# A two-layer decoder trunk: the norm on ScalarE, transposed activations split in PSUM, 128-row rotary scores and one-tensor roots

## The chip, the cores and the metric

The kernel runs on one core of a Trainium2 chip. A core has five engines with queues of their own: TensorE (PE, with its weight loads shown as PEld), VectorE (DVE), ScalarE (ACT), GpSimd (POOL) and SyncE (SP), which here issues most of the transfers. The metric is the device time of one execution in microseconds (us); lower is better.

## The reference

One sequence of 1024 tokens with 1024 features goes through two layers. A layer is a token mixer and a channel mixer. Both are wrapped in the same way, with a shift, a scale and a gate worked out from a vector `c`:

```
x <- LayerNorm(alpha * x + (1 + gate) * sublayer(x * (1 + scale) + shift))
```

The mixer of layer 0 is latent attention: 8 heads, queries and keys through low-rank latents, each head with 128 plain and 64 rotary dimensions, and the rotary key shared by all heads:

```python
s = (jnp.einsum('bqhd,bkhd->bhqk', qn, k_nope)
     + jnp.einsum('bqhr,bkr->bhqk', qp, k_pe)).astype(jnp.float32) * scale
s = jnp.where(causal, s, jnp.float32(-1e30))
p = jax.nn.softmax(s, axis=-1).astype(v.dtype)
return jnp.einsum('bhqk,bkhd->bqhd', p, v)
```

The mixer of layer 1 is a diagonal complex state-space layer (S5): an input projection, a recurrence over the tokens, GELU, a gated unit and an output projection. The channel mixer is the same in both layers, with 4096 hidden features:

```python
a = jax.nn.relu(h @ w1 + b1)
return (a * a) @ w2 + b2
```

Everything is float32.

## The kernel before, in words

**Precision.** Every large product is made of three. A float32 operand is split into `hi`, its rounding to the format in which TensorE takes one pass, and `lo`, the rest; `mm3` (lines 77 to 80, three matmuls on L78, L79 and L80) adds hi·hi, hi·lo and lo·hi in one PSUM bank. A split is a copy into `hi` on ScalarE and a subtraction into `lo` on VectorE (`split`, L74 and L75).

**Tiling.** The 1024 tokens are eight tiles of 128 rows; tile t holds every eighth token from t. `X[t]` is a 128 x 1024 tile in SBUF, the running activation. For a product over features the activation must be transposed: `hT[I]` is a pair (hi, lo) of 128 x 8 x 512 tiles, features on the partitions, 8 blocks of 128 features, 512 tokens (four tiles). `T5["h"]` is the same for the input of the state-space layer.

**Order.** The program is written for a framework that schedules it: it simulates a timeline and gives each engine its own instruction order, so that the order of the program text decides among what is ready. TensorE then takes its instructions strictly in that order. The mixer and other background work are Python generators, advanced by `step(...)`; the order in which the text calls them is written by hand. PSUM has eight banks of 512 columns after the attention: two for transposes (`psT`, tag `tr`), two for `a1` (first products of the channel mixer) and four for `mm` (output products).

**Stages on the timeline.** Setup and modulation vectors run to about 104 us. The attention runs to about 410. `score(h, i)` adds five matmuls for each stretch of keys: three by `mm3` for the plain part, and two for the rotary part (L723 and L724). For the rotary part, `st` and the tiles `kE` and `kO` are 128 rows high: 64 rows of hi and 64 of lo, in opposite order in `kE` and `kO`. L723 uses all 128 rows (hi·lo and lo·hi); L724 uses the 64 rows `r` that hold hi·hi.

Then comes the output projection of the attention, tile by tile (`o_stage`, `o_tiles`, and `o_end`, which adds the residual on L950 and calls the norm), to about 507. The channel mixer `mlp(0, ...)` with `finish0` follows: pairs of hidden blocks `mm1` and `mm2`, with weights loaded and split as it goes (`load1`, `load2`). From about 1222 to 1268 the last pass `mm2(js, h)` overlaps with the norm and the transposes for the state-space layer, whose input projection (`u_strip`, weights `wi` by `u_load`) follows. From 1490 the gated unit and output projection run, then `mlp(1, ...)` with `finish1` from about 1670 to the end at 2408.

**The norm.** `stats(t)` takes mean and variance of a tile on VectorE (`bn_stats`, `bn_aggr`) and makes 1/sqrt by `rsqrt` (L115 to L131): a shift, a first guess on the bits, and two refinements, all on one number per partition; the tiles `bmv` hold the mean and `bny` the root. `norm(t)` then applies (x − mean)·root in one VectorE instruction (L850). The gain and offset of the LayerNorm are in two places: folded into `acol` and `bcol` (with scale and shift), which are applied after the transpose, and in the rows `ra`, `rb`, by which GpSimd multiplies and adds (`residual`, L868 and L869) to make the next running activation.

**The transposes.** `to_hT(t, n, ...)` handles one token tile. For each half of the feature blocks it takes one PSUM bank, transposes four 128 x 128 blocks by TensorE (L857), applies `acol` and `bcol` by four ScalarE instructions from PSUM into an SBUF tile `ht` (L861), copies `ht` to `hi` (L864: on VectorE for the first half, on ScalarE for the second) and subtracts into `lo` on VectorE (L865). `half_dst` says where the result goes.

In layer 0, tiles 0 to 3 are transposed one by one as their norms are done; after the eighth, the loop near L1340 does tiles 4 to 7 with `step(mixer, t > 5)` between them. In `finish0` each tile is transposed, updated and stored to memory (`x_d`) when its norm is done. In layer 1, four tiles are done after tile 3 and four after tile 7. At the end, `finish1` handles the last eight tiles: 0 to 5 by `accumulate` (L841 is the addition in `stats`, L824 the one in `accumulate`), `norm` and `residual`; 6 and 7 by four instructions on VectorE (L1494, L1495), so that the last stores leave early.

Of the kernel before, what the change touches and what calls it, by code (L numbers as in the profile page):

```python
# [9 lines left out]
F32 = mybir.dt.float32  # L10
F32R = mybir.dt.float32r
I32 = mybir.dt.int32
AF = mybir.ActivationFunctionType
ALU = mybir.AluOpType
# [25 lines left out]
def kernel(  # L40
# [29 lines left out]
    def f32(ap):  # L70
        return ap.bitcast(F32)
# [43 lines left out]
    def rsqrt(v, y, tmp, ti):  # L115

        def vyy():
            if v.shape[-1] == 1:
                V.scalar_tensor_tensor(tmp, v, y, y, ALU.mult, ALU.mult)  # L119
            else:  # L120
                V.tensor_tensor(tmp, v, y, ALU.mult)
                V.tensor_tensor(tmp, tmp, y, ALU.mult)

        V.tensor_scalar(ti, v.bitcast(I32), 1, None, ALU.logical_shift_right)
        V.tensor_scalar(y.bitcast(I32), ti, -1.0, 1597463007.0, ALU.mult, ALU.add)
        vyy()
        V.scalar_tensor_tensor(y, tmp, -3.0, y, ALU.add, ALU.mult)
        vyy()
        V.scalar_tensor_tensor(tmp, tmp, -40.0 / 3.0, tmp, ALU.add, ALU.mult)
        V.tensor_scalar(tmp, tmp, 80.0, -3.0 / 256.0, ALU.add, ALU.mult)  # L130
        V.tensor_tensor(y, y, tmp, ALU.mult)  # L131
# [574 lines left out]
    def score(h, i):  # L706
        I = i // 4
        w = (i + 1) * 128
        ps = ps_s[i % 2].tile([128, 1024], F32, tag="s", name="s")
        qsl = slice((i % 4) * 128, (i % 4) * 128 + 128)  # L710
        qh, ql = Q[h, I]
        st = ST[h, I]
        for cc in range((w + 511) // 512):
            n = min(512, w - 512 * cc)
            if n == 128:
                n = 256
            o = ps[:, 512 * cc:512 * cc + n]
            kh, kl = K_[h, cc]
            mm3(o, qh[:, qsl], ql[:, qsl], kh[:, 0:n], kl[:, 0:n], True, False)
            ks, kx = (kE, kO) if h % 2 == 0 else (kO, kE)  # L720
            r = slice(0, 64) if h % 2 == 0 else slice(64, 128)
            ksl = slice(512 * cc, 512 * cc + n)
            PE.matmul(o, st[:, qsl], ks[:, ksl], start=False, stop=False)  # L723
            PE.matmul(o, st[r, qsl], kx[r, ksl], start=False, stop=True)  # L724
        d = ps[:, i * 128:i * 128 + 128]
        V.tensor_tensor(d, d, cmask, ALU.add)
        mx = ap3.tile([128, 4], F32, tag="mx", name="mx", bufs=4)
        V.reduce_max(mx[:, 0:1], ps[:, 0:w], axis=AX.X)
        V.tensor_scalar(mx[:, 1:2], mx[:, 0:1], -SM_SCALE, None, ALU.mult)
        p = ap3.tile([128, w], F32, tag=f"p{i}", name="p", bufs=1)  # L730
        S.activation(p, ps[:, 0:w], AF.Exp, bias=mx[:, 1:2], scale=SM_SCALE, accum_out=mx[:, 2:3])
        V.reciprocal(mx[:, 3:4], mx[:, 2:3])
        if i < 2:
            P.tensor_scalar(p, p, mx[:, 3:4], 0.0, ALU.mult, ALU.add)
        else:
            S.activation(p, p, AF.Copy, scale=mx[:, 3:4])
        PT[h, i] = p
# [94 lines left out]
    def stats(t, add=None):  # L832

        st = cst.tile([128, 2, 6], F32, tag="bst", name="bst", bufs=2)
        mv = cst.tile([128, 2], F32, tag="bmv", name="bmv", bufs=2)
        y = cst.tile([128, 4], F32, tag="bny", name="bny", bufs=2)
        ti = cst.tile([128, 1], I32, tag="bni", name="bni", bufs=2)
        for h in range(2):
            xh = X[t][:, h * 512:h * 512 + 512]
            if add is not None:  # L840
                V.tensor_tensor(xh, xh, add[h], ALU.add)  # L841
            V.bn_stats(st[:, h], xh)
        V.bn_aggr(mv, st.rearrange("p a b -> p (a b)"))
        V.tensor_scalar(y[:, 0:1], mv[:, 1:2], LN_EPS, None, ALU.add)
        rsqrt(y[:, 0:1], y[:, 1:2], y[:, 2:3], ti)
        return mv[:, 0:1], y[:, 1:2]

    def norm(t):

        V.tensor_scalar(X[t], X[t], *stats(t), ALU.subtract, ALU.mult)  # L850

    def to_hT(t, n, wp, dst, tile=None):

        for k0 in (0, 4):
            ps = (tile or tr_tile)()
            for k in range(4):
                PE.transpose(ps[:, k * 128:k * 128 + 128], X[t][:, (k0 + k) * 128:(k0 + k + 1) * 128], ident)  # L857
            h = wp.tile([128, 4, 128], F32, tag="r2", name="ht", bufs=4)
            for k in range(4):
                a, b, src = acol[:, n, k0 + k:k0 + k + 1], bcol[:, n, k0 + k:k0 + k + 1], ps[:, k * 128:k * 128 + 128]  # L860
                S.activation(h[:, k], src, AF.Identity, bias=b, scale=a)  # L861
            for hi, lo, view in dst(t, k0):
                hv = view(h)
                (S.activation(hi, hv, AF.Copy) if k0 else V.tensor_copy(hi, hv))  # L864
                V.tensor_tensor(lo, hv, f32(hi), ALU.subtract)  # L865

    def residual(t, ra, rb):
        P.tensor_tensor(X[t], X[t], ra, ALU.mult)  # L868
# [19 lines left out]
    def out_weight(wp, src, gate, k, hi, lo, eng=None):  # L888
# [2 lines left out]
        SY.dma_start(r, src[k * 128:(k + 1) * 128, :])  # L891
        (eng or V).tensor_tensor(r, r, gate, ALU.mult)
        split(hi, lo, r)

    def half_dst(A):
        def dst(t, k0):
            hi, lo = A[t // 4]
            sl = slice((t % 4) * 128, (t % 4) * 128 + 128)
            return [(hi[:, k0:k0 + 4, sl], lo[:, k0:k0 + 4, sl], lambda h: h)]
        return dst  # L900

    def o_tiles(lhs, w, k_outer=False):

# [43 lines left out]
    def o_end(t, ps):  # L947
        for h in range(2):
            xh = X[t][:, h * 512:h * 512 + 512]
            V.scalar_tensor_tensor(xh, xh, ALPHA, ps[h], ALU.mult, ALU.add)  # L950
        norm(t)
        if t < 4:
            to_hT(t, 0, wp, half_dst(hT))
            residual(t, ra, rb)


# [120 lines left out]
    for t in range(2, 8):  # L1077
        ps = o_tiles([nxt], WO.__getitem__, t == 7)[0]
        if t < 7:
            nxt = o_stage(t + 1)  # L1080
            o_end(t, ps)
    hT[1] = [pa1.tile([128, 8, 512], F32R, tag="pa", name="hT") for _ in range(2)]
    for p_ in wo_p[::-1]:
        p_.release()
    pb = pool("pb", bufs=4)
# [246 lines left out]
    def finish0(t, ps):  # L1332
        accumulate(t, ps)
        if t == 0:
            step(bg, 1000)
            T5["rows"] = res_rows(wp, ln_ffn_g[0], ln_ffn_b[0])
            q = [p_.tile([128, 8, 512], F32R, tag=g, name="h5") for p_, g in ((pa2, "pa"), (pa2, "pa"), (pa1, "pa"), (pb, "pb"))]
            T5["h"] = [q[0:2], q[2:4]]
        norm(t)
        to_hT(t, 1, wp, half_dst(T5["h"]))  # L1340
        residual(t, *T5["rows"])
        SY.dma_start(x_d[t], X[t])
        if t == 5:
            u_load(0)

    mixer = mlp(0, hT, cont, gffn, wp, bg, finish0, w1x, pace=0.6)
    next(mixer)
    o_end(7, ps)
    for t in range(4, 8):
        to_hT(t, 0, wp, half_dst(hT), mm_half)  # L1350
        residual(t, ra, rb)
        step(mixer, t > 5)
    step(mixer, 100)


# [125 lines left out]
    def finish1(t, ps):  # L1481
        if t == 0:
            T5["rows"] = res_rows(wp, ln_ffn_g[1], ln_ffn_b[1], al=1.0)
        g, b = T5["rows"]
        if t < 6:
            accumulate(t, ps)
            norm(t)
            residual(t, g, b)
            SY.dma_start(outr[t], X[t])
            return  # L1490
        mu, rs = stats(t, ps)
        for h in range(2):
            sl = slice(h * 512, h * 512 + 512)
            V.scalar_tensor_tensor(X[t][:, sl], X[t][:, sl], mu, g[:, sl], ALU.subtract, ALU.mult)  # L1494
            V.scalar_tensor_tensor(X[t][:, sl], X[t][:, sl], rs, b[:, sl], ALU.mult, ALU.add)  # L1495
            SY.dma_start(outr[t][:, sl], X[t][:, sl])
# [3 lines left out]
    for t0, n in ((0, 3), (3, 1), (4, 1), (5, 1), (6, 1), (7, 1)):  # L1500
        for t, ps in zip(range(t0, t0 + n), o_tiles([z_of(t) for t in range(t0, t0 + n)], WO.__getitem__, n > 1)):
            accumulate(t, ps)
            norm(t)
            if t % 4 == 3:
                hT[t // 4] = [pb.tile([128, 8, 512], F32R, tag="pb", name="hT") for _ in range(2)]
                if t == 7:
                    cont = containers(pa_tiles([128, 4096], F32R, "ct"))
                    w1x = tuple(wp.tile([128, 8, 128], F32R, tag=g, name="w1x", bufs=1) for g in ("k4", "a4"))
                    mixer = mlp(1, hT, cont, gffn, wp, iter(()), finish1, w1x)
                    next(mixer)  # L1510
                for t_ in range(t - 3, t + 1):
                    to_hT(t_, 2, wp, half_dst(hT), mm_half if t == 7 else None)
                    residual(t_, ra, rb)
                    step(mixer, t_ > 5)
    step(mixer, 100)
    for p_ in (pb, wp, psM, psA, psT, pa2, xp, pa1, drm, cst):
        p_.release()
# [31 lines left out]
```

## Time and profile before

| | |
|---|---|
| three runs | 2406.59, 2409.71 (median), 2413.19 us |
| the profiled execution | 2409.98 us |
| its span, from the first to the last instruction | 2408.0 us |
| mean granted TensorE clock | 0.971 |
| TensorE busy | 2276.5 us (95%), 11039 matmuls |
| VectorE busy | 1522.6 us (63%), 2660 instructions |
| ScalarE busy | 816.9 us (34%), 1457 instructions |
| GpSimd busy | 555.3 us (23%), 550 instructions |
| memory traffic | 190.88 MB read, 34.54 MB written, mean 94 GB/s |

The profile is of one execution. Busy times are the sums of the instructions' durations on an engine. In the lines shown below, a line of a timeline begins with the start and the duration in us, then the engine, the source line (L857), the operation, output <- inputs with their names, and in brackets the idle time before it and what ended it. A line of waits reads: who <- whom, the microseconds waited in all, how often, the longest. A line by source has minimum, median and maximum duration in ns. A line of the costliest groups has the count, the busy time in us, the mean ns of one, and the idle time before them.

### The profile page before, as it was taken

What the parts mean: (1) busy time and instruction counts of PE and PEld (TensorE: products, weight loads), DVE (VectorE), ACT (ScalarE), POOL (GpSimd) and SP (SyncE); (2) the same over time, 40 slices, a digit from 0 to 9 for tenths busy, and PEclk for the clock granted to TensorE, in tenths of its full rate; (3) what the DMA queues carried; (4) which work ended last, traced back from release to release, by engine and by line L of the source; (5) the groups of instructions that cost most, each with busy time, mean ns of one, the idle gap of its engine ahead of it and who ended that gap; (6) DMA issues with size and microseconds to landing.
All of it is one profiled execution on the core that took longest, in us unless ns stands there. A gap on an engine that the chain in (4) does not pass through costs nothing. (4 is left out here: it accounts for less than half of the span.)

```text
span 2408.0 us, 29142 instructions
## 1 busy us (share of the span) xinstructions
PE 2276.5 (95%) x11039; PEld 1885.7 (78%) x11039; DVE 1522.6 (63%) x2660; ACT 816.9 (34%) x1457; POOL 555.3 (23%) x550
## 2 busy tenths in 40 slices
PE   7799998889999999999996999998999999999995
PEld 6666776767888888888886998877788888888884
DVE  8777677977767766666467436379444444444439
ACT  3466665432222333333233233324222222222220
POOL 5623557430000234333024111015000000000004
PEclk9899999989999999999997999999899999999998
DMA  7211224126453344446114545330121111111201
GB/s 255 68 50 56 69 62 158 70 70 198 154 155 110 92 123 142 123 119 161 48 49 158 156 153 173 114 97 20 60 62 44 44 53 44 61 45 36 62 27 70
DMA packets 191289, 229.41 MB, mean 95 GB/s; under 512 B 45329, under 2 KB 136732, under 8 KB 189102
## 3 DMA queue, kind: packets, MB, share of 16 engines
q1 hardware_dynamic: 186270, 214.98, 29.1%
q0 software_dynamic: 3840, 12.59, 1.7%
q8 instruction: 86, 1.41, 0.2%
q14 instruction: 53, 0.43, 0.1%
q10 hardware_dynamic: 1040, 0.00, 0.0%
HBM read 190.88 MB, written 34.54 MB: 94 GB/s over the span
## 5 line engine op out<-in xcount | busy, mean ns | idle before, releaser
L824 DVE TENSOR_TENSOR X<-X,mm 128x512 f32<-128x512 f32 x490 | 330.4, 683 | 269.5 <-PE mm L80 265.7
L868 POOL TENSOR_TENSOR X<-X,ra 128x1024 f32<-128x1024 f32 x30 | 79.0, 2636 | 909.8 <-DVE X L850 667.9
L78 PE MATMUL mm<-pb 128*128 128x512 f32 x512 | 203.9, 399 | 5.4 <-DVE X L824 5.3
L78 PE MATMUL mm<-ct 128*128 128x512 f32 x512 | 199.4, 390 | 1.5 <-DVE X L824 1.5
L79 PE MATMUL mm<-pb 128*128 128x512 f32 x512 | 200.3, 391 | 0.0
L80 PE MATMUL mm<-pb 128*128 128x512 f32 x512 | 200.3, 391 | 0.0
L79 PE MATMUL mm<-ct 128*128 128x512 f32 x512 | 199.7, 390 | 0.0
L80 PE MATMUL mm<-ct 128*128 128x512 f32 x512 | 198.5, 389 | 0.0
L78 PE MATMUL a<-hT,ct 128*128 128x512 f32 x496 | 194.3, 392 | 2.9 <-DVE ct L1018 2.9
L78 PE MATMUL a<-hT,pb 128*128 128x512 f32 x496 | 194.9, 393 | 0.0
L1015 ACT ACTIVATE a<-a,vt 128x512 f32<-128x512 f32 x128 | 83.3, 651 | 327.5 <-PE a L80 327.4
L80 PE MATMUL a<-hT,pb 128*128 128x512 f32 x496 | 194.3, 392 | 0.0
L80 PE MATMUL a<-hT,ct 128*128 128x512 f32 x496 | 193.9, 391 | 0.0
L79 PE MATMUL a<-hT,ct 128*128 128x512 f32 x496 | 193.9, 391 | 0.0
L79 PE MATMUL a<-hT,pb 128*128 128x512 f32 x496 | 193.8, 391 | 0.0
L995 DVE TENSOR_TENSOR w2r<-w2r,gffn 128x1024 f32<-128x1024 f32 x64 | 83.0, 1297 | 138.5 <-DMA w2r<-in_mlp_w_dram 138.5
L78 PEld LDWEIGHTS mm<-pb 128*128 128x128 f32 x512 | 96.4, 188 | 27.3 <-DVE X L824 7.4
L78 PEld LDWEIGHTS mm<-ct 128*128 128x128 f32 x512 | 96.3, 188 | 21.7 <-DVE X L824 1.9
L80 PEld LDWEIGHTS mm<-pb 128*128 128x128 f32 x512 | 96.4, 188 | 20.4
L79 PEld LDWEIGHTS mm<-ct 128*128 128x128 f32 x512 | 96.4, 188 | 20.1
L78 PEld LDWEIGHTS a<-hT,ct 128*128 128x128 f32 x496 | 93.8, 189 | 23.2 <-DVE ct L1018 3.6
L80 PEld LDWEIGHTS mm<-ct 128*128 128x128 f32 x512 | 96.2, 188 | 20.0
(476 smaller groups left out, 5390.1 us busy)
## 6 DMA issues: line engine op xcount, KB each, us to landing
w1r<-in_mlp_w_dram SPq DMA_DIRECT2D x64, 512.0 KB, 4.7
w2r<-in_mlp_w_dram SPq DMA_DIRECT2D x64, 512.0 KB, 4.5
pt<-prm_d SPq DMA_DIRECT2D x16, 1536.0 KB, 7.6
prm_d<-cb SPq DMA_DIRECT2D x80, 128.0 KB, 2.4
wm<-in_mod_mix_w_dram SPq DMA_DIRECT2D x8, 1024.0 KB, 11.7
mb<-in_mod_ffn_w_dram POOLq DMA_DIRECT2D x32, 256.0 KB, 3.1
mb<-in_mod_ffn_w_dram SPq DMA_DIRECT2D x32, 256.0 KB, 2.9
mr<-in_mod_ffn_w_dram SPq DMA_DIRECT2D x32, 256.0 KB, 3.4
```

What stands on the lines that cost most here:

```text
L78: PE.matmul(ps, lh, rh, start=start, stop=False)
L79: PE.matmul(ps, lh, rl, start=False, stop=False)
L80: PE.matmul(ps, ll, rh, start=False, stop=stop)
L824: V.tensor_tensor(xh, xh, ps[h], ALU.add)
L868: P.tensor_tensor(X[t], X[t], ra, ALU.mult)
L995: V.tensor_tensor(r, r, gate, ALU.mult)
L1015: S.activation(ps, ps, AF.Relu, bias=vt2[:, l * 32 + j:l * 32 + j + 1])
```

## The change

1. **Rotary scores (L724).** The second rotary matmul takes all 128 rows of `st` and `kx` instead of the 64 rows `r`; the other 64 rows add the product lo·lo.
2. **Roots.** For one number per partition, `rsqrt` is written with `tensor_scalar` alone: one tensor, and the other operands as pointers to one number per partition. For eight numbers per partition it stays as it was, in the older form with two tensors.
3. **Norm.** `scaled_rows` makes −mean·root by a small VectorE instruction and then applies root·x − mean·root by one ScalarE instruction. `finish1` uses it for its tiles 0 to 5, with the addition of the last products inside `stats`.
4. **Transposes.** `to_hT` takes a group of g = 2 or 4 tiles of tokens. A PSUM bank holds 4/g feature blocks of all g tiles. ScalarE applies `acol` and `bcol` in place in PSUM, one instruction for each feature block, then copies the bank to `hi`; VectorE subtracts from PSUM into `lo`. The SBUF tile `ht` is gone.
5. **Order.** In layer 0, tiles 0 to 3 are transposed together after tile 3, tiles 4 and 5 after tile 6, tiles 6 and 7 after tile 7, with one `step(mixer)` ahead; `hT[1]` is taken at tile 6. In `finish0`, tiles are transposed, updated and stored in pairs. In layer 1 one `step(mixer)` comes ahead of the transposes after tile 7, which go in the pairs (4, 5) and (6, 7), without steps between.

```diff
@@ rsqrt
+        if v.shape[-1] == 1:
+            V.tensor_scalar(tmp, y, y, v, ALU.mult, ALU.mult)
+            V.tensor_scalar(y, tmp, -3.0, y, ALU.add, ALU.mult)
+            V.tensor_scalar(tmp, y, y, v, ALU.mult, ALU.mult)
+            V.tensor_scalar(tmp, tmp, -40.0 / 3.0, tmp, ALU.add, ALU.mult)
+            V.tensor_scalar(tmp, tmp, 80.0, -3.0 / 256.0, ALU.add, ALU.mult)
+            V.tensor_scalar(y, y, tmp, None, ALU.mult)
+            return
@@ score
-            r = slice(0, 64) if h % 2 == 0 else slice(64, 128)
             PE.matmul(o, st[:, qsl], ks[:, ksl], start=False, stop=False)
-            PE.matmul(o, st[r, qsl], kx[r, ksl], start=False, stop=True)
+            PE.matmul(o, st[:, qsl], kx[:, ksl], start=False, stop=True)
@@ norm, to_hT
-        V.tensor_scalar(X[t], X[t], *stats(t), ALU.subtract, ALU.mult)
+        scaled_rows(t, *stats(t))
+
+    def scaled_rows(t, mu, rs):
+        nm = cst.tile([128, 1], F32, tag="bnm", name="bnm", bufs=2)
+        V.tensor_scalar(nm, mu, rs, -1.0, ALU.mult, ALU.mult)
+        S.activation(X[t], X[t], AF.Identity, bias=nm, scale=rs)
+
+    def to_hT(ts, n, A, tile=None):
+
+        g = len(ts)
+        m = 4 // g
+        hi, lo = A[ts[0] // 4]
+        c0 = (ts[0] % 4) * 128
+        for k0 in range(0, 8, m):
             ps = (tile or tr_tile)()
+            for k in range(m):
+                for i, t in enumerate(ts):
+                    o = (k * g + i) * 128
+                    PE.transpose(ps[:, o:o + 128], X[t][:, (k0 + k) * 128:(k0 + k + 1) * 128], ident)
+            for k in range(m):
+                q = ps[:, k * g * 128:(k + 1) * g * 128]
+                S.activation(q, q, AF.Identity, bias=bcol[:, n, k0 + k:k0 + k + 1], scale=acol[:, n, k0 + k:k0 + k + 1])
+            v = ps.rearrange("p (k f) -> p k f", k=m)
+            ks, cs_ = slice(k0, k0 + m), slice(c0, c0 + 128 * g)
+            S.activation(hi[:, ks, cs_], v, AF.Copy)
+            V.tensor_tensor(lo[:, ks, cs_], v, f32(hi[:, ks, cs_]), ALU.subtract)
@@ o_end
         norm(t)
-        if t < 4:
-            to_hT(t, 0, wp, half_dst(hT))
+        ts = {3: range(4), 6: (4, 5), 7: (6, 7)}.get(t, ())
+        if t == 7:
+            step(mixer)
+        if ts:
+            to_hT(ts, 0, hT, mm_half if t == 7 else None)
+        for t in ts:
             residual(t, ra, rb)
@@ finish0
-        to_hT(t, 1, wp, half_dst(T5["h"]))
-        residual(t, *T5["rows"])
-        SY.dma_start(x_d[t], X[t])
+        if t % 2:
+            to_hT((t - 1, t), 1, T5["h"])
+            for t_ in (t - 1, t):
+                residual(t_, *T5["rows"])
+                SY.dma_start(x_d[t_], X[t_])
...
     o_end(7, ps)
-    for t in range(4, 8):
-        to_hT(t, 0, wp, half_dst(hT), mm_half)
-        residual(t, ra, rb)
-        step(mixer, t > 5)
     step(mixer, 100)
@@ finish1
-            accumulate(t, ps)
-            norm(t)
+            scaled_rows(t, *stats(t, ps))
             residual(t, g, b)
@@ layer 1
                     next(mixer)
-                for t_ in range(t - 3, t + 1):
-                    to_hT(t_, 2, wp, half_dst(hT), mm_half if t == 7 else None)
-                    residual(t_, ra, rb)
-                    step(mixer, t_ > 5)
+                    step(mixer)
+                for ts in ((4, 5), (6, 7)) if t == 7 else (range(4),):
+                    to_hT(ts, 2, hT, mm_half if t == 7 else None)
+                    for t_ in ts:
+                        residual(t_, ra, rb)
```

More of the change, by code (lines that the diff above doesn't have):

```diff
@@ L117, in vyy @@
         def vyy():
[L118 to L122, printed above, removed]
+            V.tensor_tensor(tmp, v, y, ALU.mult)
+            V.tensor_tensor(tmp, tmp, y, ALU.mult)
         V.tensor_scalar(ti, v.bitcast(I32), 1, None, ALU.logical_shift_right)
         V.tensor_scalar(y.bitcast(I32), ti, -1.0, 1597463007.0, ALU.mult, ALU.add)
+        if v.shape[-1] == 1:
[6 more added lines that the diff above has]
+            return
         vyy()
@@ L848, in norm @@
     def norm(t):
-        V.tensor_scalar(X[t], X[t], *stats(t), ALU.subtract, ALU.mult)
-    def to_hT(t, n, wp, dst, tile=None):
-        for k0 in (0, 4):
-            ps = (tile or tr_tile)()
[L856 to L865, printed above, removed]
+        scaled_rows(t, *stats(t))
[9 more added lines that the diff above has]
+        for k0 in range(0, 8, m):
+            ps = (tile or tr_tile)()
+            for k in range(m):
[9 more added lines that the diff above has]
+            V.tensor_tensor(lo[:, ks, cs_], v, f32(hi[:, ks, cs_]), ALU.subtract)
     def residual(t, ra, rb):
@@ L893, in out_weight @@
         split(hi, lo, r)
[L895 to L900, printed above, removed]
     def o_tiles(lhs, w, k_outer=False):
@@ L1080 @@
             nxt = o_stage(t + 1)
+            if t == 6:
+                hT[1] = [pa1.tile([128, 8, 512], F32R, tag="pa", name="hT") for _ in range(2)]
             o_end(t, ps)
-    hT[1] = [pa1.tile([128, 8, 512], F32R, tag="pa", name="hT") for _ in range(2)]
     for p_ in wo_p[::-1]:
```

## Prediction

> **What bounds the kernel now.** I read the busy times and the granted clock on the first page, then the busy times by stage, then the waits of TensorE, then the timelines of the places that those waits name.
>
> ```profile
> span 2408.0 us, 29142 instructions
> PE 2276.5 (95%) x11039; PEld 1885.7 (78%) x11039; DVE 1522.6 (63%) x2660; ACT 816.9 (34%) x1457; POOL 555.3 (23%) x550
> PEclk9899999989999999999997999999899999999998
> ```
>
> TensorE is busy for 95% of the span. A change gains only if it shortens TensorE's own stream or closes one of its gaps. The clock's digits (tenths of full speed in 40 slices of the span) are at 9, and at 7 or 8 in a few slices. By stage:
>
> ```profile
> 104.00:410.00 306.00, 292.82 (x1400) 215.12 (x1399) 224.34 (x499) 191.91 (x376) 148.90 (x162) 0.97 0.25 76
> ...
> 486.00:545.00 59.00, 48.48 (x218) 40.01 (x217) 43.15 (x65) 24.18 (x51) 23.01 (x9) 0.88 0.25 77
> ...
> 1222.00:1325.00 103.00, 82.87 (x473) 73.63 (x472) 81.39 (x154) 37.53 (x92) 41.66 (x18) 0.87 0.31 109
> 1600.00:1712.00 112.00, 96.32 (x436) 78.97 (x435) 92.91 (x156) 39.24 (x88) 46.72 (x18) 0.91 0.14 43
> 2336.00:2408.00 72.00, 45.85 (x202) 37.30 (x200) 58.59 (x129) 4.63 (x7) 29.60 (x12) 0.85 0.15 59
> ```
>
> The columns are window, length, busy TensorE, weight load, VectorE, ScalarE, GpSimd, clock. Attention (104 to 410) keeps TensorE at 96%. The four other windows are where layers and sub-layers hand over and where the kernel ends: there the clock is 0.85 to 0.91 and TensorE misses 10 to 26 us. Who it waits for:
>
> ```profile
> PE mm L857 <- DVE X L850: 21.0, 2, 10.5
> PE a L79 <- DVE wi L75: 18.6, 3, 7.9
> ...
> PE tr L857 <- DVE X L850: 3.2, 1, 3.2
> ```
>
> Nearly all are VectorE, at the norm (L850) and at a split (L75). VectorE in the first of these windows:
>
> ```profile
> 507.43 2.60 DVE L75 TENSOR_TENSOR pb<-w1r,pb 128x1024 fp32r<-128x1024 f32 x1
> ...
> 510.07 3.30 DVE L75 TENSOR_TENSOR pb<-w1r,pb 128x1024 fp32r<-128x1024 f32 x1
> ...
> 513.36 2.55 DVE L864 CAST hT<-ht 128x512 fp32r<-128x512 f32 x1
> ...
> 515.95 2.77 DVE L865 TENSOR_TENSOR hT<-ht,hT 128x512 fp32r<-128x512 f32 x1
> ...
> 518.82 2.13 DVE L119 SCALAR_TENSOR_TENSOR bny<-bny 128x1 f32<-128x1 f32 x1
> ...
> 522.01 2.29 DVE L127 SCALAR_TENSOR_TENSOR bny<-bny 128x1 f32<-128x1 f32 x1
> ```
>
> An operation on one number per partition took 2.13 and 2.29 us. Other rows by their source line give minimum, median and maximum in ns:
>
> ```profile
> L119 DVE SCALAR_TENSOR_TENSOR bny<-bny x64: 203/219/2307, 436.6 to 2402.6; 128x1 f32<-128x1 f32 x64
> L130 DVE TENSOR_SCALAR bny<-bny x32: 94/147/166, 439.1 to 2403.0; 128x1 f32<-128x1 f32 x32
> L868 POOL TENSOR_TENSOR X<-X,ra x30: 2334/2474/3382, 446.0 to 2389.7; 128x1024 f32<-128x1024 f32 x30
> L1018 DVE TENSOR_TENSOR ct<-a,ct x64: 678/684/695, 1693.4 to 2346.6; 128x512 fp32r<-128x512 f32 x64
> L850 DVE TENSOR_SCALAR X<-X,bmv,bny x30: 761/807/2285, 439.4 to 2388.8; 128x1024 f32<-128x1024 f32 x30
> ```
>
> The long cases last about as long as one GpSimd residual (L868, 2.47 us). The forms that reach it read two SBUF tensors, or copy SBUF to SBUF. L130, which has constants only, never exceeds 0.166 us; L1018, which reads PSUM and one SBUF tensor, never exceeds 0.695. So a VectorE instruction of the first kind waits out a running GpSimd residual. The change replaces such forms in the root (L119, L127), the split (L864, L865) and the norm (L850).
>
> **The change part by part.** (1) Rotary scores. 96 matmuls of 64 rows become 128 rows.
>
> ```profile
> 311.43 0.39 PE L80 MATMUL s<-kh,ql 128*128 128x512 f32 x1
> 311.66 0.40 PE L723 MATMUL s<-kO,stO 128*128 128x512 f32 x1
> 311.99 0.50 PE L724 MATMUL s<-kE,stO 64*128 64x512 f32 x1
> 312.42 0.50 PE L78 MATMUL s<-kh,qh 128*128 128x512 f32 x1
> ...
> L724 PE MATMUL s<-kO,stE x48: 379/492/579, 105.4 to 348.2; 64*128 64x512 f32 x24, 64*128 64x256 f32 x16, 64*128 64x384 f32 x8
> ```
>
> Starts of equal matmuls lie 0.23 apart (311.43 to 311.66). Into the 64-row one it is 0.33, out of it 0.43: 0.10 + 0.20 = 0.30 us lost. The row gives 48 for half of the heads, half of them narrower; as a loss at a change of shape it is nearly the same for these, 96 × 0.29 = 28 us (if it went with the columns, about 23). In this stage VectorE is at 224/306 = 73% and ScalarE at 63%, so TensorE leads; but some waits of TensorE for them will reopen. I take −22, bounds −28 and 0.
>
> (2) Roots. Six instructions on [128,1] with pointer scalars, all one tensor each, replace six of which five read two. Unblocked they cost the same (0.15 to 0.22). The gain comes in the hand-overs, below, and is not counted here. The two [128,8] roots keep their path.
>
> (3) Norm on ScalarE. It removes 30 × 0.81 us from VectorE, adds a 0.15 us product there, and adds an activation of 1024 columns.
>
> ```profile
> L736 ACT ACTIVATE p<-p,mx 128x1024 f32<-128x1024 f32 x8 | 9.3, 1158 | 0.3 <-DVE mx L732 0.2
> L1015 ACT ACTIVATE a<-a,vt 128x512 f32<-128x512 f32 x128 | 83.3, 651 | 327.5 <-PE a L80 327.4
> ...
> L861 ACT ACTIVATE ht<-tr,bcol,acol 128x128 f32<-128x128 f32 x128 | 47.0, 469 | 73.2 <-PE tr L857 70.3 <-DVE bny L125 2.8
> ```
>
> The nearest row is L736 at 1.16 us, with one pointer; with two I take 1.25. On the path a norm is therefore 1.25 − 0.81 + 0.15 plus some 0.1 of hand-off, 0.7 us longer. Three lie on TensorE's path (the last tile of each hand-over): +2, bounds −4 (three times the 1.5 by which the longest L850 exceeds the median) and +21 (all 30 late by 0.7). What is queued behind it on ScalarE is the Relu, Square and Copy of an MLP block, with TensorE a block ahead.
>
> The Trainium skill, page "ScalarE: Activation LUTs", section "Rules for kernel authors", says to use VectorE rather than ScalarE for additions and products. By that rule the move itself is the loss, as in rival R6 below, with 19 us more. The rows agree on the bare duration, 0.81 against 1.16, yet here VectorE is the engine that TensorE waits for.
>
> (4) Transposes. A bank now gets an activation of 128·g columns in place, a 512-column Copy, and a VectorE subtraction from PSUM. ScalarE does 0.65 (L1015; 0.94 as two activations of a pair of tiles, twice L861) + 0.65 for each bank, against 4 × 0.47 and every second time a Copy before, so it is relieved; VectorE loses the casts. But a bank is now held until the subtraction ends: 0.65 + 0.65 + 0.68 = 2.0 us (2.3 for a pair), against 4 × 0.47 = 1.9 before. With two banks in turn, TensorE's four transposes (half of the 1.94 us of the eight at 529.78 below, at the low clock; some 0.5 at the full one) wait where nothing else is ready. I take +5 for the 48 banks, a tenth of a microsecond each, bounds 0 and +40 (0.85 each).
>
> (5) Order at the hand-overs.
>
> ```profile
> 529.78 1.94 PE L857 MATMUL mm<-ident,X 128*128 128x128 f32 x8 [10.52 <-DVE X L850]
> ...
> 531.94 0.63 PE L79 MATMUL a<-hT,pb 128*128 128x512 f32 x1
> 532.37 0.63 PE L80 MATMUL a<-hT,pb 128*128 128x512 f32 x1
> ...
> 1687.56 1.94 PE L857 MATMUL mm<-ident,X 128*128 128x128 f32 x8 [10.48 <-DVE X L850]
> ...
> 1694.09 0.79 PE L78 MATMUL a<-hT,ct 128*128 128x512 f32 x1 [2.89 <-DVE ct L1018]
> ```
>
> Layer 0: waits 3.2 + 10.5, then matmuls 0.43 apart (531.94 to 532.37) instead of 0.23 for a dozen, about 2.3. With the roots and splits unblocked (four of the rows above, 2.1 to 2.8, shrink to 0.2 to 0.7, some 8 us) and the mixer's first blocks queued ahead, I take −10, bounds −16 and 0. What is late next is the last tile's norm and its pair of transposes. MLP to state-space layer: the three waits for wi are 18.6 in sum, and the cold clock adds about 3; the weight split of L75 itself still reads two SBUF tensors and its transfer comes when a tile of x is free, which pairing delays by one tile: −15, bounds −22 and 0. Layer 1: 10.5 + 2.9 and 3 for the clock: −11, bounds −16 and 0. The residuals of the even tiles move behind the odd ones on GpSimd, and with them 4 stores on SP's queue; the stores land behind the next tile's matmuls, 24 × 0.23 = 5.5 us in the last pass, and cost nothing while those run, or one residual of 2.5 at the end without them.
>
> (6) The end.
>
> ```profile
> 2382.94 0.39 PE L80 MATMUL mm<-ct 128*128 128x512 f32 x1
> ...
> 2389.80 5.49 DVE L1494 SCALAR_TENSOR_TENSOR X<-X,bmv,ra 128x512 f32<-128x512 f32 x2
> ...
> 2398.14 0.69 DVE L842 BATCH_NORM_STATS2 bst<-X 128x6 f32<-128x512 f32 x1
> ...
> 2400.57 0.14 DVE L124 TENSOR_SCALAR bni<-bny 128x1 int32<-128x1 int32 x1
> ...
> 2403.42 1.42 DVE L1495 SCALAR_TENSOR_TENSOR X<-X,bny,rb 128x512 f32<-128x512 f32 x2
> ```
>
> The last matmul ends at 2383.3 and the span 24.7 us later. The last tile alone needs an addition and statistics (0.7 each, 0.2 to join the halves), the root (2.9 from L124 to L1495, eight instructions that take turns with tile 6), two pairs of products (1.4 each) and the last store (2408.0 − 2404.8 = 3.2): 10.5. The rest is tile 6 behind blocked operations: two of L1494 took 5.49, where two of L1495 take 1.42. Unblocked, the end is 10.5 to 19 after the last matmul: −14, bounds −6 and −14.
>
> Sum: −22 + 2 + 5 − 10 − 15 − 11 − 14 = −65. The profiled execution took 2409.98 us (2.0 outside the span); 2409.98 − 65 = 2345. The median of the runs, 2409.71, is the same within 0.3 us.
>
> **The rivals.** R1, the hand-overs stay: the wait for L850 becomes a wait for the same tile's activation, or for a transpose bank. For it: one tile's chain of statistics, root, norm, transposes and split is still serial. Against it: 8 us of the 10.5 were other work. The three hand-over terms (36) vanish: 2381.
>
> R2, the rotary gain is hidden, because scores wait for the softmax of two tiles before. For it: VectorE at 73% there, and 96 matmuls that end sooner ask for it sooner. Against: TensorE at 96%. 2345 + 22 = 2367.
>
> R3, the pointer forms wait for GpSimd as well: L850 has two pointer scalars and one tensor, and reached 2.285. Then half of the hand-overs (18) and of the end (7) is lost: 2370.
>
> The Trainium skill, page "SBUF — State Buffer", section "Who interferes with whom", states that VectorE shares a port with GpSimd in operations with two SBUF inputs or in its two-port modes. The 695 of L1018 agrees; L850's maximum leaves the pointer form open.
>
> R4, slower. Each of the 48 banks waits for its subtraction, which stands in VectorE's queue behind an operation that waits out a residual (2.4 us): a bank is then held 2.3 + 2.4 = 4.7, half of that with two banks in turn is 2.35, less the 0.5 that the transposes take: 1.85 × 48 = 89, so −65 − 5 + 89 = +19: 2429. It decides from 70/48 = 1.46 us per bank. Against it: matmuls of another stage stand between most banks. R5: what is gained at one place is lost at the next wait, and nothing moves: 2410. R6, each norm holds its tile up by the 0.7 of step 3: 2345 + 30 × 0.7 − 2 = 2364; for it, one tile's norm is always on the way to its transposes; against it, TensorE has a tile's 5.5 us of matmuls under most.
>
> **How the numbers follow.** Forecast 0.50, R1 0.17, R2 0.09, R3 0.06, R6 0.04, R5 0.06, R4 0.08. Faster 0.50 + 0.17 + 0.09 + 0.06 + 0.04 = 0.86, same 0.06, slower 0.08; the bound of 0.3%, 7 us, is about what a measurement of this kernel can tell from no change. The forecast's own range is 2322 to 2366, within the bounds of its terms (0.45 of the 0.50); up to 2388 come R1, R2, R3 and R6, 0.81 together.
>
> **What the profile after would show.** L724 with 128 rows, and starts 0.23 apart around it; attention about 22 us shorter; no root instruction over 0.3 us; no wait of 10 us before transposes; the end 11 us after the last matmul. I am wrong if transposes wait for subtractions or if attention keeps its 306 us.

## The result, and the profile after

The changed kernel takes 2383.66 us (median of four runs, 2378.32 to 2386.33) against 2411.45 us before (four runs), a ratio of 0.9884 with a 95% interval of 0.9858 to 0.9910: 28 us faster, where 65 were forecast. The profiled execution took 2378.32 us, 2376.0 of them in the span.

The first page of the changed kernel:

```profile
span 2376.0 us, 29109 instructions
...
PE 2259.4 (95%) x11039; PEld 1883.3 (79%) x11039; DVE 1437.7 (61%) x2636; ACT 835.3 (35%) x1399; POOL 557.2 (23%) x550
...
PEclk9799999989999999999998999999999999999998
```

TensorE's busy time fell by only 17 us, though the rotary matmuls alone should have given 28; VectorE lost 85 us. The stages that answer to those of before (window, length, busy TensorE, weight load, VectorE, ScalarE, GpSimd, clock):

```profile
104.00:379.00 275.00, 256.38 (x1403) 216.62 (x1404) 218.37 (x497) 191.68 (x378) 152.01 (x162) 0.97 0.27 84
455.00:509.00 54.00, 40.95 (x178) 32.66 (x178) 32.31 (x48) 26.16 (x44) 44.24 (x17) 0.86 0.24 78
1192.00:1292.00 100.00, 84.58 (x466) 72.80 (x465) 59.62 (x149) 44.88 (x79) 39.09 (x18) 0.88 0.36 119
1569.00:1681.00 112.00, 96.78 (x434) 77.88 (x433) 71.75 (x149) 41.81 (x65) 45.51 (x17) 0.94 0.13 43
2312.00:2376.00 64.00, 46.20 (x203) 37.76 (x201) 46.23 (x129) 12.00 (x13) 29.54 (x12) 0.88 0.17 66
```

The same attention matmuls fit into 275 us instead of 306. At the hand-overs VectorE works less (60 us instead of 81 in the third row, 72 instead of 93 in the fourth), but TensorE misses about as much as before: 13, 15 and 15 us. Its waits:

```profile
PE a L78 <- DVE ct L1029: 11.9, 1, 11.9
PE tr L872 <- DVE h L879: 9.6, 6, 2.8
PE a L78 <- ACT hT L878: 9.2, 2, 6.0
...
PE a L78 <- DVE pb L1029: 4.5, 1, 4.5
...
PE a L79 <- DVE wi L75: 1.9, 1, 1.9
```

The waits for the norm are gone, and that for `wi` went from 18.6 to 1.9. In their place stand the split of the first hidden blocks (L1029, which was L1018) and the splits of the transposed activations (L878, L879).

Where the 32 us of the two spans came from is read off instructions that both kernels have: the last rotary matmul, the last hidden block's split of each channel mixer, and the end. In the kernel before, the first two are

```profile
L724 PE MATMUL s<-kE,stO x48: 378/467/789, 139.3 to 385.1; 64*128 64x512 f32 x24, 64*128 64x256 f32 x16, 64*128 64x384 f32 x8
```

```profile
L1018 DVE TENSOR_TENSOR pb<-a,pb x64: 672/684/695, 530.1 to 1229.0; 128x512 fp32r<-128x512 f32 x64
```

and 2346.6 for the second mixer (the prediction shows that row). After the change:

```profile
L728 PE MATMUL s<-kE,stO x48: 278/366/628, 134.8 to 354.2; 128*128 128x512 f32 x24, 128*128 128x256 f32 x16, 128*128 128x384 f32 x8
```

```profile
L1029 DVE TENSOR_TENSOR pb<-a,pb x64: 675/684/693, 486.5 to 1200.3; 128x512 fp32r<-128x512 f32 x64
L1029 DVE TENSOR_TENSOR ct<-a,ct x64: 678/684/693, 1656.4 to 2323.2; 128x512 fp32r<-128x512 f32 x64
```

So the lead is 385.1 − 354.2 = 30.9 us at the end of the attention, 28.7 at the end of the first mixer, 23.4 at the end of the second, and 32.0 at the end of the span. Between the attention and the last pass the change lost 7.5 us, where 29 (36 less the 7 that steps 3 and 4 cost) were to be won.

Part of that loss is in no wait. Within the second mixer, 300 us in which TensorE is never idle, of the kernel before and of the changed one:

```profile
1800.00:2100.00 300.00, 300.00 (x1325) 248.43 (x1324) 138.12 (x179) 76.16 (x109) 0.00 (x0) 1.00 0.16 49
```

```profile
1800.00:2100.00 300.00, 300.00 (x1312) 246.09 (x1311) 138.76 (x177) 77.04 (x109) 0.00 (x0) 1.00 0.16 50
```

1325 matmuls against 1312, with the same clock of 1.00: 226.4 against 228.7 ns each, 1% more, in a stretch in which the change alters no instruction. What it alters there is the place of tiles. The framework fills SBUF from two sides, left and right, and its addresses can be read in the program that it builds. The two tiles `bnm` of the norm's offset stand early on the left side, each rounded up to 32 bytes a partition, and everything allocated after them there stands 64 bytes higher (`pb` at 63776 instead of 63712), while the tiles of the right side stay (`ct` at 131040). A first product of a channel mixer takes one operand from each side.

### The profile page after: what moved, and what is told of

Read it like the earlier page. It is cut to its first block, busy times and chain, and to the rows that moved or that the text cites. A ratio compares the mean times of both kernels' runs of the same rounds, so it can differ in the third digit from the quotient of the medians.

```text
span 2376.0 us, 29109 instructions
## 1 busy us (share of the span) xinstructions
PE 2259.4 (95%) x11039; PEld 1883.3 (79%) x11039; DVE 1437.7 (61%) x2636; ACT 835.3 (35%) x1399; POOL 557.2 (23%) x550
## 4 chain that ended last, share of the span: by engine, by line
PE 84%; DVE 7%; issue 2%; ACT 2%; DMA 2%; POOL 2%; SPq 0%; DVEq 0%; ACTq 0%; POOLq 0%
PE a L79 12%; PE a L78 12%; PE a L80 12%; PE mm L78 12%; PE mm L79 12%; PE mm L80 12%; PE mm L1390 1%; PE tr L872 1%; DMA qs<-qr 1%; PE tr L751 1%; PE tr L1284 1%; DMA mb<-in_mod_ffn_w_dram 1%; POOL mb L564 1%; POOL mb L565 0%; PE a L1417 0%
## 5 line engine op out<-in xcount | busy, mean ns | idle before, releaser
L828 DVE TENSOR_TENSOR X<-X,mm 128x512 f32<-128x512 f32 x478 | 323.8, 684 | 307.9 <-PE mm L80 303.6
L78 PE MATMUL a<-hT,ct 128*128 128x512 f32 x496 | 195.3, 394 | 11.9 <-DVE ct L1029 11.9
L1026 ACT ACTIVATE a<-a,vt 128x512 f32<-128x512 f32 x128 | 83.5, 652 | 347.3 <-PE a L80 347.3
L78 PE MATMUL a<-hT,pb 128*128 128x512 f32 x496 | 197.9, 399 | 4.5 <-DVE pb L1029 4.5
L79 PE MATMUL a<-hT,pb 128*128 128x512 f32 x496 | 196.9, 397 | 0.0
L80 PE MATMUL a<-hT,pb 128*128 128x512 f32 x496 | 196.9, 397 | 0.0
L1006 DVE TENSOR_TENSOR w2r<-w2r,gffn 128x1024 f32<-128x1024 f32 x64 | 85.5, 1335 | 124.3 <-DMA w2r<-in_mlp_w_dram 124.3
L78 PEld LDWEIGHTS a<-hT,pb 128*128 128x128 f32 x496 | 93.9, 189 | 27.1 <-DVE pb L1029 5.0
L78 PEld LDWEIGHTS mm<-pb 128*128 128x128 f32 x512 | 96.1, 188 | 21.4 <-issue 0.5
```

Of the source, the lines that this page charges most:

```text
L78: PE.matmul(ps, lh, rh, start=start, stop=False)
L79: PE.matmul(ps, lh, rl, start=False, stop=False)
L80: PE.matmul(ps, ll, rh, start=False, stop=stop)
L828: V.tensor_tensor(xh, xh, ps[h], ALU.add)
L1006: V.tensor_tensor(r, r, gate, ALU.mult)
L1026: S.activation(ps, ps, AF.Relu, bias=vt2[:, l * 32 + j:l * 32 + j + 1])
```

## The experiments

Times are compared as ratios to the kernel before on the same chip, since its median was 2410 to 2417 us from chip to chip. A ratio's difference of 0.001 is 2.4 us. The expectations name absolute times; where the chips differ, the ratio decides.

**e1: the offset in a column that was free.**

```diff
-        nm = cst.tile([128, 1], F32, tag="bnm", name="bnm", bufs=2)
         V.tensor_scalar(nm, mu, rs, -1.0, ALU.mult, ALU.mult)
...
-        return mv[:, 0:1], y[:, 1:2]
+        return mv[:, 0:1], y[:, 1:2], y[:, 3:4]
```

> The changed kernel, with the offset of the norm kept in the unused fourth column of the tile bny instead of in tiles of its own, so that all later tiles of the left side of SBUF stand 64 bytes lower, where they stood before the change. Theory A (the 64-byte shift makes TensorE's matmuls slower where stationary and moving operand stand differently to 128 bytes): the first products of the channel mixers start 227 ns apart again instead of 229 to 233, the two mixers win 6 to 7 us each, in all 13 us against the changed kernel, some 2371 us. Theory B (the 1% more is the clock of that execution, or load on SBUF by the new instructions): pitch and time stay as in the changed kernel, 2384 us, within 5.

2362.13 us, ratio 0.9799 (0.9784 to 0.9814). That is 0.0085 below the changed kernel, 20 us. The same 300 us of e1:

```profile
1800.00:2100.00 300.00, 300.00 (x1326) 248.47 (x1325) 140.28 (x181) 76.14 (x109) 0.00 (x0) 1.00 0.15 48
```

**e2: the move alone.** The kernel before with two unused 4-byte tiles in the same place.

```diff
+        if t == 0 and not sh:
+            sh.append(cst.tile([128, 1], F32, tag="bnm", name="bnm", bufs=2))
+            V.memset(sh[0], 0.0)
```

> The kernel before, with two unused tiles of four bytes a partition taken where the change takes those for the norm's offset; nothing else. Theory A: slower by about 13 us, some 2423 us, pitch of the first products 229 to 233 ns. Theory B: the same within 3 us, pitch 227.

2430.65 us, ratio 1.0076 (1.0055 to 1.0097): 18 us slower (20 in medians), though nothing is computed differently.

```profile
1800.00:2100.00 300.00, 300.00 (x1312) 246.08 (x1311) 139.43 (x178) 77.02 (x109) 0.00 (x0) 1.00 0.16 50
```

Together e1 and e2 show theory A's cause, from both sides; its size was set too low (13). The first products of the two mixers start 229.9 (`ct`) and 233.4 ns (`pb`) apart on average in e2, against 226.7 and 227.0 before; the second products lose some too (`ct` 227.9 against 226.7), and the state-space layer's products slow down as well (those of `wg` 233.3 against 226.7).

**e8, e11, e12: moves of 128, 256 and 512 bytes**, with `bufs=4`, `8` and `16` in the lines of e2.

> The kernel before with unused tiles that move the left side of SBUF by 128 bytes instead of 64. If it is the position to 128 bytes that counts: pitch of 227 ns and the time of before, 2410 us, within 4. If any move, or less room, makes it slower: 2420 to 2430 as with 64 bytes.

> The kernel before, left side of SBUF moved by 256 bytes. Moves of 64 and 128 cost 1.6% of the pitch of the first products. If it goes by the distance of both operands to 512 bytes (256 before the change, 192 and 128 in the moved ones), this one (0) is as slow or slower, pitch 229 to 240 ns. If 256 is the period: 227.

> The kernel before, moved by 512 bytes. With a period of 512 bytes: pitch 227 and the time of before. If any move makes it slower: 229 and more, 2420 to 2435 us.

The 128-byte move is slow, ratio 1.0068 (1.0044 to 1.0092), which refutes the 128 bytes that I had named; the moves of 256 and 512 bytes are not (2417.94 and 2418.76 us in one run each, beside 2416.56). Moved by 128, then by 256:

```profile
1800.00:2100.00 300.00, 300.00 (x1303) 244.42 (x1303) 137.40 (x175) 77.98 (x111) 0.00 (x0) 1.00 0.16 50
```

```profile
1800.00:2100.00 300.00, 300.00 (x1326) 248.47 (x1325) 139.41 (x179) 77.81 (x111) 0.00 (x0) 1.00 0.16 50
```

1325 matmuls with no move, 1312 with 64 bytes, 1303 with 128, 1326 with 256, 1325 with 512. The five points fit a period of 256 bytes. The distance from `pb` to `ct` before, 131040 − 63712 = 67328 bytes, is 263 times 256, but every run moved the left side alone: whether the distance counts, or the left side's own address, is not shown. Why the hardware behaves so no run shows either.

**e3: rotary rows alone.** The two lines of `score` in the diff.

> The kernel before with the 128-row rotary matmuls alone. If the loss is the change of the row count, as the starts 0.33 and 0.43 us apart say: 28 us less, about 2382 us, the attention shorter by 28. If the 30 us by which the attention became shorter came partly from elsewhere, or the scores wait for the softmax: 2390 or more.

2384.21 us, ratio 0.9890 (0.9873 to 0.9906): 26 us. In the changed kernel the starts around the second rotary matmul:

```profile
302.72 0.39 PE L80 MATMUL s<-kh,ql 128*128 128x512 f32 x1
302.95 0.40 PE L727 MATMUL s<-kE,stE 128*128 128x512 f32 x1
303.19 0.40 PE L728 MATMUL s<-kO,stE 128*128 128x512 f32 x1
303.42 0.40 PE L78 MATMUL o<-ph,vh 128*128 128x512 f32 x1
```

They lie 0.23 to 0.24 apart; the 0.33 and 0.43 are gone. In e3's profile the last rotary matmul starts at 356.4 us, against 385.1 before.

**e4: roots alone.** The first hunk of the diff.

> The kernel before with the one-tensor roots alone. If blocked roots set the time at the hand-overs: no root instruction over 0.3 us, the waits for the norm of 10.5 us become some 6, 5 to 15 us less, 2395 to 2405. If the residuals on GpSimd now block the weight split and the gate's product instead, and these are as late: the roots are short and the time is within 5 us of before, 2405 to 2412.

2398.54 us, ratio 0.9956 (0.9940 to 0.9972): 11 us. No pointer form on one number per partition waits for GpSimd; the longest of the slowest of them, in the changed kernel, is 0.275 us:

```profile
L124 DVE TENSOR_SCALAR bny<-bny x32: 256/272/275, 407.5 to 2368.6; 128x1 f32<-128x1 f32 x32
```

But in e4's profile the waits for the norm stay (two of them 21.2 us in sum, before 21.0) and those for `wi` go from 18.6 to 14.7. Where the gain lies is read off the same instructions as above, the last rotary matmul and the last hidden block's split:

```profile
L729 PE MATMUL s<-kE,stO x48: 378/491/792, 143.1 to 391.1; 64*128 64x512 f32 x24, 64*128 64x256 f32 x16, 64*128 64x384 f32 x8
```

```profile
L1023 DVE TENSOR_TENSOR ct<-a,ct x64: 679/684/695, 1691.5 to 2343.8; 128x512 fp32r<-128x512 f32 x64
```

The attention, which e4 doesn't change, ends 6.0 us later in this profile (391.1 against 385.1; in the profiles of e2, e8, e11 and e12, which have the old rotary rows too, at 388.4 to 390.5). From there to the last split e4 takes 8.8 us less than before (1952.7 against 1961.5), and behind it 7.8 us less. So the roots gained at the hand-overs about as much as at the end. Of the 8.8 us, 5.3 come between the two mixers, where the waits for `wi` shrank by 3.9 us; the waits for the norm were not shortened.

**e7: e1 with the transposes, splits and order of before.** `to_hT`, `half_dst`, `o_end`, `finish0` and the two loops as before the change.

> The kernel e1 with transposes, splits and order of before: tile by tile, through the SBUF tile ht, so the kernel before with rotary rows, roots and ScalarE norm. If each part's gain stands by itself (26 for the rotary rows, 12 for the roots, 10 left for norm, transposes and order): 2362 to 2372 us. If grouping the transposes costs at the hand-overs what it gains: the same as e1, 2362. By the prediction's sum of the hand-overs it would have to lose some 30: 2390.

2380.65 us, ratio 0.9849 (0.9828 to 0.9870). This misses all three forecasts; on a chip whose kernel before takes 2410 us the ratio gives 2374, just above the first. So transposes and order together win 0.0050, 12 us (6 to 18 by the intervals); rotary rows and roots make 0.9846 by themselves (0.9890 and 0.9956), and the ScalarE norm adds nothing to them that could be told from zero (8 us either way). In e7 the wait for the norm is merely renamed, from VectorE to ScalarE:

```profile
PE mm L865 <- ACT X L858: 22.5, 2, 11.3
```

**e6: e1 with the norm on VectorE**, and **e13: e9 with the norm on ScalarE** (e9 is below).

```diff
-        scaled_rows(t, *stats(t))
+        V.tensor_scalar(X[t], X[t], *stats(t)[:2], ALU.subtract, ALU.mult)
```

The same is done for tiles 0 to 5 in `finish1`.

> The kernel e1 with the norm as one VectorE instruction again. Theory T: ScalarE loses 30 instructions of 1.24 us and the hand-overs become shorter by some 5 us, 2357. Theory P: the norm is again a VectorE instruction that can wait for GpSimd, nothing on ScalarE mattered: 0 to 5 us more, 2362 to 2367.

> The kernel e9 (residuals of the hand-overs on VectorE) with the norm on ScalarE as in e1. Before (ratio 0.9799 for e1, 0.9767 for e6) the place of the norm made no clear difference. If the ScalarE norm frees 0.8 us a tile of the VectorE queue that TensorE waits for: 5 us or more less than e9, a ratio of 0.969 or less. If its longer way (1.24 + 0.2 us and two engines) costs as much: within 0.0025 of e9's 0.9709. If it costs 0.7 us a tile: 0.979.

e6: 2360.71 us, ratio 0.9767 (0.9743 to 0.9790), against 0.9799 for e1: 8 us less, 1 to 14 by the intervals, so this pair leans to the norm on VectorE. e13: 2351.16 us, ratio 0.9715 (0.9695 to 0.9734), against 0.9709 for e9: the same, to within 9 us. Taken together the two pairs leave open whether the ScalarE norm costs some microseconds; neither shows a gain from it.

**e5: e1 without the residuals of the three hand-overs.** The calls of `residual` in `o_end`, `finish0` and the loop of layer 1 are left out.

> The kernel e1 without the residuals on GpSimd (multiply by ra, add rb) behind the transposes of both layers and in finish0; those of finish1 stay. This leaves that part of the computation out. Theory P (at the hand-overs the residuals, now two to four tiles in a row, hold up VectorE's weight splits and gate products, which read two SBUF tensors, and with them the split of the first hidden blocks): the waits of 4.8, 9.9 and 3.2 us ahead of the first products fall below 3, the weight instructions of 3.2 us fall to 1.2, 15 to 25 us less than e1, 2337 to 2347 us. Theory T (ScalarE's queue sets it, in which norm and transposed activations stand between the Relu, Square and Copy of a hidden block): within 5 us of e1, 2357 to 2367.

2334.53 us, ratio 0.9661 (0.9638 to 0.9684): 0.0138 below e1, 33 us. This is theory P, and more than it asked for. Theory T falls as the main cause; e6 leaves it a share of some microseconds. How it works is seen on VectorE in the changed kernel, ahead of the 11.9 us wait in layer 1:

```profile
1639.09 1.83 DVE L1006 TENSOR_TENSOR w2r<-w2r,gffn 128x1024 f32<-128x1024 f32 x1
...
1641.11 3.18 DVE L1006 TENSOR_TENSOR w2r<-w2r,gffn 128x1024 f32<-128x1024 f32 x1
...
1644.27 3.34 DVE L75 TENSOR_TENSOR ct<-w2r,ct 128x1024 fp32r<-128x1024 f32 x1
...
1647.72 3.17 DVE L75 TENSOR_TENSOR ct<-w2r,ct 128x1024 fp32r<-128x1024 f32 x1
...
1654.16 2.33 DVE L1006 TENSOR_TENSOR w2r<-w2r,gffn 128x1024 f32<-128x1024 f32 x1 [1.90 <-DMA w2r<-in_mlp_w_dram]
1656.42 0.68 DVE L1029 TENSOR_TENSOR ct<-a,ct 128x512 fp32r<-128x512 f32 x1
```

and on GpSimd at that time:

```profile
1639.80 3.40 POOL L883 TENSOR_TENSOR X<-X,rb 128x1024 f32<-128x1024 f32 x1
1643.17 6.64 POOL L882 TENSOR_TENSOR X<-X,ra 128x1024 f32<-128x1024 f32 x2
1649.77 3.32 POOL L883 TENSOR_TENSOR X<-X,rb 128x1024 f32<-128x1024 f32 x1
```

The weight work (gate product L1006, split L75) reads two SBUF tensors and takes 3.2 to 3.3 us instead of the 1.2 it takes undisturbed, each time that a residual runs; the residual takes 3.3 instead of 2.4 in return. The last root instructions, the small product for the norm and the split at 1656.42, for which TensorE waits, stand behind this in VectorE's queue. Not all of the 11.9 us are of this kind: the block's last matmul ends at 1645.3, and its three ScalarE instructions (L1026 to L1028, 1.9 us of work) are done only at 1650.1, because transposed activations stand between them; and 1.90 us of the rest are a wait for the transfer of `w2r`. The change made root and activation split immune and left the weights as they were. With the residuals gone the longest weight split of the second mixer falls from 3364 ns in e1 to 1227; first e1, then e5:

```profile
L75 DVE TENSOR_TENSOR ct<-w2r,ct x32: 1212/1225/3364, 1633.8 to 2304.4; 128x1024 fp32r<-128x1024 f32 x32
```

```profile
L75 DVE TENSOR_TENSOR ct<-w2r,ct x32: 1215/1222/1227, 1608.9 to 2274.1; 128x1024 fp32r<-128x1024 f32 x32
```

e5 also takes away the results that others wait for (in e1 ScalarE waits twice for a residual, 4.2 and 3.7 us, and the stores of `x_d` wait), so its 33 us are what these residuals cost in all, not the blocking alone.

**e9: e6 with the hand-overs' residuals on VectorE.** The six residuals of `finish1` stay on GpSimd.

```diff
     def residual(t, ra, rb):
-        P.tensor_tensor(X[t], X[t], ra, ALU.mult)
-        P.tensor_tensor(X[t], X[t], rb, ALU.add)
+        V.tensor_tensor(X[t], X[t], ra, ALU.mult)
+        V.tensor_tensor(X[t], X[t], rb, ALU.add)
```

> The kernel e6 (norm on VectorE, no shift) with the residuals of the hand-overs on VectorE instead of GpSimd, two instructions of some 1.2 us for each tile; finish1 keeps GpSimd. If what costs is that VectorE's two-tensor instructions stand still while GpSimd runs (2.4 us each, 4.9 a tile), then VectorE is better off with 2.4 us of its own a tile: 5 to 15 us less than e6, 2345 to 2356. If VectorE is simply short of time at the hand-overs: 5 to 15 us more, 2366 to 2376.

2345.29 us, ratio 0.9709 (0.9684 to 0.9734), 0.0058 below e6, 14 us. VectorE takes over 48 instructions, and TensorE still waits for it less (ahead of layer 1's first hidden blocks 3.4 us instead of e6's 11.5):

```profile
L881 DVE TENSOR_TENSOR X<-X,ra x24: 1215/1219/1226, 467.5 to 1642.5; 128x1024 f32<-128x1024 f32 x24
```

1.22 us each against 2.41 on GpSimd. Against the changed kernel the ratio is 0.9709/0.9884 = 0.982. Of these 0.018, 0.0085 come from the move that e9 doesn't have. By the intervals, e9 is faster than both kernels of this case.

**e10: e6 with the residuals of layers 0 and 1 held back** until a later hidden block is there. `held_residuals` is called once in each layer, behind the transposes of tile 7, in place of the calls of `residual`.

```diff
+    def held_residuals(ra, rb):
+        step(mixer, 2)
+        for t in range(8):
+            S.activation(vt1[:, 126:127], f32(cont[2][1][:, 0, 0:1]), AF.Identity, bias=X[t][:, 0:1])
+            residual(t, ra, rb)
```

> The kernel e6 with the sixteen residuals of the output projections of layers 0 and 1 held back until the second hidden block of the mixer is there (each waits for a small ScalarE read of its tile that also reads that block); those of finish0 stay. Theory P: the layer 0 and layer 1 hand-overs get what leaving out the residuals gave them (some 10 and 8 us), 10 to 18 us less than e6, 2343 to 2351 us. Rival: the residuals block as many weight splits ten microseconds later, and TensorE waits there: within 4 us of e6.

2361.20 us, ratio 0.9777 (0.9743 to 0.9812): no different from e6 (10 us either way by the intervals). The time is the rival's. Its mechanism, the same 80 us of GpSimd work blocking as much a little later, is seen in layer 0 alone: from the attention to the last split of the first mixer the profile of e10 takes 4.0 us more than that of e6, and the longest split of a first weight (`pb<-w1r`) goes from 2806 to 3410 ns. From there to the last split of the second mixer it takes 5.9 us less. That the blocking explains the whole is not shown.

**e14: e9 with the residuals of `finish1` on VectorE too.** Its six calls use `residual` as e9 has it.

> The kernel e9 with the six residuals of finish1 on VectorE as well. If the last tiles still wait for VectorE instructions that GpSimd's residuals block: the end comes 2 to 4 us earlier, ratio 0.969 to 0.970. If six times 2.4 us more on VectorE make the last tile late: 2 to 10 us later.

2348.97 us, ratio 0.9716 (0.9701 to 0.9730): the same as e9. The products of the last two tiles no longer wait (0.74 us each instead of 2.3), but the residuals now stand ahead of them in the queue. From the last matmul to the end it is 22.3 us in e14 and 18.9 in e9.

## Why the prediction was wrong

The time, 2384, lies outside the forecast's own range (2322 to 2366). That it lies beside rival R1 (2381) is luck: in R1 the hand-overs gain nothing, and here they gained some 8 us, while a loss of 20 that no rival names came on top. Point by point:

1. **Rotary rows: −22 forecast, −26 measured (e3).** Right, and the method was right: starts read off the timeline, times 96, gave 28. The discount for waits that would reopen was not needed.
2. **Roots: right in mechanism.** Rival R3 fell (0.275 us at most; two of the six instructions take 0.27, a little over the 0.15 to 0.22 that were expected). By themselves they won 11 us, in e4's profile about half at the hand-overs and half at the end.
3. **Norm: +2 forecast, nothing measurable found.** R6 (+19) is excluded by e13 against e9, and by e1 against e6, which still allow 9 and 14. The norm costs 1.24 us on ScalarE, as estimated:

```profile
L859 ACT ACTIVATE X<-X,bnm,bny x30: 1227/1243/1258, 409.4 to 2353.7; 128x1024 f32<-128x1024 f32 x30
```

 The Trainium skill, page "ScalarE: Activation LUTs", section "Rules for kernel authors", advises VectorE for additions and products. The bare durations agree (0.81 us on VectorE before, 1.24 on ScalarE); what that does to the time these runs don't resolve.
4. **Hand-overs: −36 forecast (with steps 3 and 4, −29), some −8 measured once the move is taken out.** This is the step that failed. In e1, which has no move, the lead is 32.9 us at the end of the attention and 40.4 at the end of the second mixer (385.1 − 352.2 and 2346.6 − 2306.2), so 7.5. Against the profiles of e11 and e12, which compute what the kernel before computes, it is 10 and 13 us:

```profile
L728 PE MATMUL s<-kE,stO x48: 274/387/522, 137.2 to 352.2; 128*128 128x512 f32 x24, 128*128 128x256 f32 x16, 128*128 128x384 f32 x8
```

```profile
L1028 DVE TENSOR_TENSOR ct<-a,ct x64: 678/684/695, 1645.9 to 2306.2; 128x512 fp32r<-128x512 f32 x64
```

 The prediction saw that VectorE waits for GpSimd, listed the blocked instructions, and counted the change's four as the whole; only for `wi` did it say that the weight split stays as it is. The first two rows that it quoted, the weight splits at 507.43 and 510.07 of 2.60 and 3.30 us, are of a kind that the change does not touch. With these in the queue a shorter norm only brings the next waiter forward. The prediction's own sign of being wrong came as well: transposes wait for subtractions (L872 for L879), 9.6 us in six waits, where step 4 had 5 for all 48 banks; in e5 it is 3.6, so that the residuals are behind most of this too. R4's 89 us are far off. Taking the residuals out (e5) brought 33 us, more than the 21 that are missing here: the right cause, at the wrong end of it. The Trainium skill, page "SBUF — State Buffer", section "Who interferes with whom", states that a VectorE instruction with two SBUF inputs contends with a GpSimd instruction that reads SBUF. e5 agrees: the weight split's maximum falls from 3364 to 1227 ns.
5. **The end: −14 forecast, −8.6 measured** (32.0 − 23.4, from the last hidden block's split on). From the last matmul to the end, as the prediction counts it, the time fell from 24.7 to 17.8 us, by 6.9. The four products L1503 read two SBUF tensors and still stood behind the last residuals on GpSimd; the first two took 4.72 us, where two of L1504 take 1.42:

```profile
2354.63 4.72 DVE L1503 SCALAR_TENSOR_TENSOR X<-X,bmv,ra 128x512 f32<-128x512 f32 x2
...
2370.19 1.42 DVE L1504 SCALAR_TENSOR_TENSOR X<-X,bny,rb 128x512 f32<-128x512 f32 x2
```

 The prediction took the whole end as unblocked, the far side of its own bounds.
6. **The place of the tiles: not in the prediction, +20 (e1, e2).** Every edit was priced by its instructions. That a tile of four bytes moves all later ones had no term, and no row of the profile before could have shown it.

In sum: −65, −4 for the rotary rows, +21 for the hand-overs, +5 for the end, +20 for the move: −23, against −28 measured. The other 5 are not assigned; they are within what the attention alone differed between the profiles of kernels with 128 rotary rows (its last matmul at 352.2 to 359.1 us).

## What to carry to other kernels

When one engine's instructions wait for another's, take out the cause for once (here: leave out the GpSimd work) before pricing the immunisation of single victims; what is left in the queue sets the time. A GpSimd operation that stops VectorE's two-tensor instructions while it runs can be cheaper on VectorE itself, at half the duration. When a stage that no edit touches slows down by a per cent, compare the addresses of its operands before looking for a new wait.

## What the runs showed of the hardware

Matmuls whose stationary operand comes from one side of SBUF and whose moving operand from the other slowed down when one side was moved by 64 or 128 bytes. Over 300 us of the second mixer, second products included, starts lay 226.4 ns apart as before, and 228.7 and 230.2 with these moves; moves of 256 and 512 bytes cost nothing (1326 and 1325 matmuls against 1325). Over this kernel a 64-byte move costs 18 to 20 us, more than the roots alone (11) or the transposes with their order (12) brought.

VectorE instructions on one number per partition with pointer scalars are not held up by GpSimd (0.275 us at most), while the norm of 1024 columns, with pointer scalars as well, was held up to 2.29 us in the kernel before; the form alone does not decide it.
